# A stream's cached values move next to the following unit's stream scores

## The chip, the cores and the metric

One NeuronCore of one Trainium2 chip runs the kernel. The metric is the device time of one execution in microseconds (us); less is better. The engines are TensorE (PE, its weight loads PEld), VectorE (DVE), ScalarE (ACT), GpSimd (POOL) and SyncE (SP), which issues the DMAs. Products read SBUF and write PSUM.

## The reference, cut to what matters

One step of a hybrid encoder layer. A prompt of 1024 tokens and eight running streams of 16 new tokens each (128 stream tokens in all) are projected, attend in eight head groups ("units"), are gated, projected out and normalised. The streams attend to cached keys and values as well as to their own new ones:

```python
def band_attention_sample(q, k_new, v_new, k_cache, v_cache, rel_bias):   # units A0, A1
    k = jnp.concatenate([k_cache, k_new], axis=1)      # 128 cached rows, then 16 new ones
    v = jnp.concatenate([v_cache, v_new], axis=1)
    s = jnp.einsum('bqhd,bkhd->bhqk', q, k) * (q.shape[-1] ** -0.5) + rel_position_bias(...)
    p = jax.nn.softmax(s, axis=-1)
    return jnp.einsum('bhqk,bkhd->bqhd', p, v)

def diff_core(q, k, v, lam, mask):                     # units B0 to B3, the streams without a mask
    s = jnp.einsum('bqhmd,bkhmd->bhmqk', q, k) * (q.shape[-1] ** -0.5)
    p = jax.nn.softmax(s, axis=-1)
    w = p[:, :, 0] - lam * p[:, :, 1]
    return jnp.einsum('bhqk,bkhe->bqhe', w, v)         # diff_post scales it by its root mean square
```

Units M0 and M1 attend to 256 memory rows only. Everything is float32.

## The kernel before, in words

The eight units run in the order M0, B0, B1, B2, B3, A0, A1, M1. For each one the loop near the end of the kernel emits: the K block (`k_block`, three column chunks, 24 steps of three products, `step`, lines 155 to 157), then the V block, a gate block and the next unit's Q block as `fill`, merged with the unit's prompt attention (`attention_b`, `attention_a`, `attention_m`). V blocks transpose their chunks (`flip` in `v_block`, line 427), and gate blocks copy theirs out at line 449 into the `t1` buffers (three), the same ones that the V chunks hold until they are transposed.

The streams' attention of a unit is a list of stages from `sample` (lines 786 to 921). For a B or A unit these are: `load_k` (512 KB into the one buffer `kc`), `score(0)`, `flip`, `product(0)`, `back`, and for B also `stat` and a DMA that brings the mean squares back. `score` spreads the queries (`qz`, on POOL), multiplies the cached keys in products of 32 weight columns, one for each quarter of the array (line 806, 8 products in the source, 16 in the trace, since a float32 product runs as two), multiplies the own keys with all 128 columns (line 811), does the softmax (`soft`, into the one buffer `se`) and issues `load_v`, which puts the cached values into the same buffer `kc`. `flip` transposes the probabilities (line 863) into `pz`. `product` multiplies them with the cached values, again in products of 32 weight columns (line 891: 16 in the trace for a B unit, 32 of half the width for an A unit), then with the own values (also line 891, 128 columns), and copies the sum out (line 894). `back` transposes that (line 901) and stores it. The stages of a unit are emitted among the steps of the next unit's K block, one after every fifth step (`EV`), and what is left of them right after that block; `finish` of the unit before (its scale factors, line 523) goes behind the first of them. Those of A1 go among its own fill.

The order on each engine is the framework's: it takes whatever is ready, by the order of emission (`high_priority` moves the streams' products 100 instructions ahead). A `manual_schedule` region fixes only the order of the PE instructions inside it; others can come in between. So in a row of 32-column products there can be others, of the prompt's attention above all (lines 476, 506, 639, 678). Buffers of one tag are given out in the order in which the tiles are made: `pt` in PSUM (two buffers; all transposes, and the sum of `product`), `ps` in PSUM (three; all scores), `p` in SBUF (six; the prompt's probabilities), `t1`.

Of the kernel before, what the change touches and what calls it, by code (L numbers as in the profile page):

```python
# [15 lines left out]
P = 128  # L16
KT = 8
NTOK = 1152
NPR = 1024
# [56 lines left out]
def hybrid_step(tc, d, o):  # L76
# [331 lines left out]
    def v_block(u, blk, out, skip):  # L408

        vts = {}  # L410
        u.vdone = 0

        def evac(c, ps):
            vt = tmp.tile([P, CH], F32, tag="t1", bufs=3)
            vts[c] = vt
            nc.scalar.copy(vt, ps)
            c0 = max(skip, c * CH)
            if c0 < (c + 1) * CH:
                nc.sync.dma_start(out[:, c0 - skip : (c + 1) * CH - skip], vt[:, c0 - c * CH :])

        def flip(c):
            if c == 0:
                u.va = op_.tile([P, KT, 2, P], F32R, tag="va")
            m = npr(c) // P
            pt = ps_t.tile([P, 3, P], F32, tag="pt")
            for t in range(3):
                nc.tensor.transpose(pt[:, t], vts[c][:, t * P : (t + 1) * P], ident)  # L427
            dst = u.va[:, 3 * c : 3 * c + m]
            if u.kind == "B":
                hi, lo, src = dst[:, :, 0], dst[:, :, 1], pt[:, 0:m]  # L430
            else:
                hi, lo, src = dst[:, :, :, 0:64], dst[:, :, :, 64:128], pt[:, 0:m].rearrange("p t (h e) -> p t h e", h=2)
            nc.scalar.copy(hi, src)
            nc.vector.tensor_tensor(out=lo, in0=src, in1=f(hi), op=ALU.subtract)
            if c == 2:
                u.sv = sp.tile([P, P], F32, tag="sv")
                nc.scalar.copy(u.sv, pt[:, 2])
            u.vdone += 1

        cs = project(blk, evac)  # L440
        items = cs[0] + cs[1][:4] + [(0.35, lambda: flip(0))] + cs[1][4:]
        return items + cs[2][:4] + [(0.35, lambda: flip(1))] + cs[2][4:], [(0.35, lambda: flip(2))]
# [44 lines left out]

    def post_b(u, po, c0, n):

        od = tmp.tile([P, n], F32, tag=f"od{n}", bufs=n // P)  # L490
        nc.scalar.copy(od, po)
        hi = tmp.tile([P, 256], F32R, tag="sqh", bufs=1)
        lo = tmp.tile([P, 256], F32R, tag="sql", bufs=1)
# [292 lines left out]
    def sample(u, kc_src, vc_src, nmask):  # L786
# [3 lines left out]
        nh = 1 if kind == "B" else 2  # L790
        st = {}

        def score(t):
            if t == 0:
                for m in range(2):
                    for par in range(2):
                        src = u.sqz[m][64 * m : 64 * m + 64].rearrange("p (a b t) -> p a b t", b=2, t=16)[:, :, par]
                        nc.gpsimd.tensor_copy(qz[m][64 * par : 64 * par + 64, :, par], src)
                st["ps"] = ps_s.tile([P, 2, 256], F32, tag="ps")
            ps = st["ps"]  # L800
            kc = st["kc"]
            with tc.high_priority(offset=SP_), tc.manual_schedule(engines={PE}):

                for m in range(2):
                    for a in range(4):
                        nc.tensor.matmul(  # L806
                            ps[32 * a : 32 * a + 32, m, P * t : P * t + P], lhsT=qz[m][:, a], rhs=kc[:, m, a],
                            start=True, stop=True)
                if kind != "M":
                    for m in range(2):  # L810
                        nc.tensor.matmul(ps[:, m, 128:256], lhsT=u.sqz[m], rhs=u.sk, start=True, stop=True)
            if t == nk - 1:
                soft()
                load_v(0)
            else:
                load_k(t + 1)

        def last(tag, shape):

# [51 lines left out]

        ew = P // nh

        def product(t):
            if t == 0:
                st["po"] = ps_t.tile([P, P], F32, tag="pt")
            po, e, vc = st["po"], st["e"], st["vc"]
# [7 lines left out]
            if kind != "M":  # L885
                for h in range(nh):
                    c = slice(h * ew, (h + 1) * ew)
                    mm.append((po[:, c], e[:, h, 0:P], u.sv[:, c], False))
            with tc.high_priority(offset=SP_), tc.manual_schedule(engines={PE}):
                for x, (out, a, b, first) in enumerate(mm):  # L890
                    nc.tensor.matmul(out, lhsT=a, rhs=b, start=first, stop=(t == nk - 1 and x >= len(mm) - (4 if kind == "M" else 1)))  # L891
            if t == nk - 1:
                st["ot"] = e[:, 1, P:256]
                nc.scalar.copy(st["ot"], po)
            else:
                load_v(t + 1)

        def back():

# [2 lines left out]
            if kind == "B":  # L902
                st["sq"] = post_b(u, pt, NPR, P)
            else:
                od = u.out[:, NPR:NTOK] if u.slot == 7 else tmp.tile([P, P], F32, tag="od128", bufs=1)
# [5 lines left out]
            ms = ps_t.tile([1, P], F32, tag="pt")  # L911
            mean_square(u, st["sq"], ms, NPR, P)

        stages = [(0.0, lambda: load_k(0))] + [(0.7, lambda t=t: score(t)) for t in range(nk)] + [(0.4, flip)]
        stages += [(1.0, lambda t=t: product(t)) for t in range(nk)] + [(0.2, back)]
# [59 lines left out]
    def q_of(u):  # L975
        return q_block(u, base[u.kind][0] + u.idx, -0.125 if u.kind == "A" else 0.125)
# [176 lines left out]

    stages = []
    late = []
    first = [q_of(units[0])] + [gate_block(next(gates)) for _ in range(NG[0])]
    for row in zip(*first):
        for part in row:
            emit(part)
    for i, u in enumerate(units):  # L1160
# [149 lines left out]
```

## Time and profile before

| what | us |
|---|---|
| median of three runs | 676.22 (675.5 to 677.12) |
| the profiled execution: its time | 675.73 |
| its span, from the first to the last instruction | 673.9 |
| PE busy | 660.9 (98%) |
| mean granted TensorE clock, share of full speed | 0.996 |
| DVE, ACT, POOL busy | 473.7, 356.3, 235.1 |

The span is 1.8 us shorter than the time of the same execution. A PE row's first two figures are its start and its duration; products overlap in the array, so what one costs is the distance to the start of the next, not its duration. A row of the timeline that ends in xN stands for N like instructions in a row.

### The profile page before, as it was taken

The numbers are of one execution on the slowest core, as the hardware profiler recorded it, in microseconds if no ns is written. First come the engines' busy times: TensorE is split into PE (matmuls) and PEld (weight loads), VectorE is DVE, ScalarE is ACT, GpSimd is POOL, SyncE is SP. The second block draws the span as 40 slices with busy tenths as digits, with TensorE's granted clock in tenths as the row PEclk, the third lists the DMA queues.
The fourth block names the chain that finished last, engine by engine and source line by source line (L and its number), as shares of the span: only waits on it lengthen the run. The fifth ranks groups of instructions, "written<-read, shape, count | busy, mean of one in ns | idle before, by whom it ended". The sixth has DMA issues, their size and how long they took to land.

```text
span 673.9 us, 12216 instructions
## 1 busy us (share of the span) xinstructions
PE 660.9 (98%) x4306; PEld 614.8 (91%) x4306; DVE 473.7 (70%) x1169; ACT 356.3 (53%) x922; POOL 235.1 (35%) x282
## 2 busy tenths in 40 slices
PE   9899999999999999999999999999999999999995
PEld 8899999999999999999999999999999998887884
DVE  4869966796569856898466516675376689897854
ACT  6748855566455655566465635666466577211000
POOL 8654212541344333541234234313324124153101
PEclk9999999999999999999999999999999999999998
DMA  8771442022312222023322122031322657974411
GB/s 279 236 226 52 143 140 72 33 80 75 96 58 83 75 100 75 25 97 127 94 68 71 52 95 75 25 118 62 127 87 95 211 173 243 318 268 148 157 62 63
DMA packets 55693, 78.91 MB, mean 117 GB/s; under 512 B 9368, under 2 KB 33232, under 8 KB 55632
## 3 DMA queue, kind: packets, MB, share of 16 engines
q1 hardware_dynamic: 55632, 78.13, 35.4%
q8 instruction: 34, 0.56, 0.3%
q14 instruction: 27, 0.22, 0.1%
HBM read 57.69 MB, written 20.42 MB: 116 GB/s over the span
## 4 chain that ended last, share of the span: by engine, by line
PE 85%; DVE 7%; DMA 4%; issue 1%; ACT 1%; SPq 1%; POOL 0%; POOLq 0%; DVEq 0%; ACTq 0%
PE pp L155 16%; PE pp L156 16%; PE pp L157 16%; PE pp L1049 8%; PE ps L1049 6%; PE pt L476 4%; PE po L639 4%; PE ps L463 4%; PE ps L464 4%; PE po L678 3%; PE pt L891 1%; PE ps L806 1%; DVE xl L219 1%; DVE p L545 1%; PE pt L427 1%
## 5 line engine op out<-in xcount | busy, mean ns | idle before, releaser
L155 PE MATMUL pp<-xh,whi 128*128 128x384 f32 x616 | 211.5, 343 | 0.2 <-DVE qa L172 0.2
L156 PE MATMUL pp<-xl,whi 128*128 128x384 f32 x616 | 209.8, 341 | 1.8 <-DVE xl L219 1.8
L157 PE MATMUL pp<-xh,wlo 128*128 128x384 f32 x616 | 209.8, 341 | 0.0
L156 PEld LDWEIGHTS pp<-xl,whi 128*128 128x128 f32 x616 | 115.9, 188 | 4.6 <-DVE xl L219 2.4
L155 PEld LDWEIGHTS pp<-xh,whi 128*128 128x128 f32 x616 | 115.9, 188 | 3.2 <-issue 0.7
L157 PEld LDWEIGHTS pp<-xh,wlo 128*128 128x128 f32 x616 | 115.9, 188 | 1.6 <-issue 0.2
L140 POOL TENSOR_TENSOR wlo<-wraw,whi 128x512 fp32r<-128x512 f32 x54 | 72.4, 1362 | 65.6 <-ACT whi L139 50.4
L605 ACT ACTIVATE p<-ps,nm 128x512 f32<-128x512 f32 (+3 forms) x96 | 55.2, 580 | 47.8 <-DVE nm L602 36.2
L463 PE MATMUL ps<-ka,qa 128*128 128x512 f32 (+4 forms) x176 | 58.7, 339 | 0.5 <-DVE nm L712 0.5
L464 PE MATMUL ps<-kl,qa 128*128 128x512 f32 (+4 forms) x176 | 57.5, 328 | 0.0
L476 PE MATMUL pt<-ident,p 128*128 128x128 f32 x332 | 54.9, 274 | 0.6 <-DVE p L545 0.5
L600 DVE TENSOR_REDUCE nm<-ps 128x1 f32<-128x512 f32 (+3 forms) x96 | 51.0, 549 | 1.6
L480 DVE TENSOR_TENSOR ptl<-pt,pth 128x512 fp32r<-128x512 f32 x56 | 38.3, 684 | 10.3 <-ACT pth L479 9.7
L479 ACT CAST pth<-pt 128x512 fp32r<-128x512 f32 x56 | 32.6, 587 | 23.1 <-PE pt L476 19.9
L720 POOL TENSOR_SCALAR p<-p,rs 128x640 f32<-128x640 f32 (+4 forms) x32 | 21.5, 676 | 64.3 <-DVE rs L719 58.7
L476 PEld LDWEIGHTS pt<-ident,p 128*128 128x128 f32 x332 | 39.7, 141 | 3.9 <-DVE p L545 0.8
L1049 PE MATMUL pp<-xh,whi 128*128 128x512 f32 (+1 forms) x96 | 36.5, 381 | 0.0
L1049 PE MATMUL pp<-xl,whi 128*128 128x512 f32 (+1 forms) x96 | 36.2, 377 | 0.0
L1049 PE MATMUL pp<-xh,wlo 128*128 128x512 f32 (+1 forms) x96 | 35.9, 378 | 0.0
L639 PE MATMUL po<-pth,va 128*128 128x256 f32 (+1 forms) x160 | 35.4, 285 | 0.0
L463 PEld LDWEIGHTS ps<-ka,qa 128*128 128x128 f32 x176 | 33.2, 189 | 2.0 <-DVE nm L712 0.7
L484 DVE TENSOR_TENSOR ptl<-pt,pth 128x256 fp32r<-128x256 f32 (+1 forms) x72 | 25.1, 352 | 13.6 <-ACT pth L483 13.0
(240 smaller groups left out, 1425.0 us busy)
## 6 DMA issues: line engine op xcount, KB each, us to landing
wraw<-in_win SPq DMA_DIRECT2D x54, 256.0 KB, 3.2
xr<-in_xT SPq DMA_DIRECT2D x12, 384.0 KB, 4.6
gates<-t SPq DMA_DIRECT2D x24, 192.0 KB, 2.1
qa<-in_xn SPq DMA_DIRECT2D x9, 512.0 KB
out_y<-qa SPq DMA_DIRECT2D x16, 256.0 KB, 2.3
mixed<-od SPq DMA_DIRECT2D x28, 128.0 KB, 1.8
p<-gates SPq DMA_DIRECT2D x7, 512.0 KB
p<-mixed SPq DMA_DIRECT2D x7, 448.0 KB
```

Source lines behind the costliest of these rows:

```text
L140: eng.tensor_tensor(out=lo[:, h], in0=raw, in1=f(hi[:, h]), op=ALU.subtract)
L155: nc.tensor.matmul(ps, lhsT=w[0][:, k], rhs=xh_[:, k], start=(k == 0), stop=False)
L156: nc.tensor.matmul(ps, lhsT=w[0][:, k], rhs=xl_[:, k], start=False, stop=False)
L157: nc.tensor.matmul(ps, lhsT=w[1][:, k], rhs=xh_[:, k], start=False, stop=(k == KT - 1))
L463: nc.tensor.matmul(ps, lhsT=u.qa[h][:, qs], rhs=u.ka[h][:, k0 : k0 + n], start=True, stop=False)
L464: nc.tensor.matmul(ps, lhsT=u.qa[h][:, qs], rhs=kl[h][:, k0 : k0 + n], start=False, stop=True)
L476: nc.tensor.transpose(pt[:, t, q * P : (q + 1) * P], p[q][:, cols[t][q] : cols[t][q] + P], ident)
L480: nc.vector.tensor_tensor(out=lo, in0=pt, in1=f(hi), op=ALU.subtract)
L600: nc.vector.tensor_reduce(out=nm[:, m, c : c + 1], in_=ps[c][:, : b - a], axis=AX.X, op=ALU.max, negate=True)
L605: nc.scalar.activation(e[:, a:b], ps[c][:, : b - a], AF.Exp, bias=nm[:, m, 0:1], accum_out=rs[:, m, c : c + 1])
L639: nc.tensor.matmul(out, lhsT=a, rhs=b, start=(g == 0 and x == 0), stop=(g == j and x == len(mm) - 1))
L1049: nc.tensor.matmul(y, lhsT=a[:, k], rhs=b[k][:, s], start=(k == 0 and x == 0), stop=(k == KT - 1 and x == 2))
```

## The change

For the B and A units the second half of the stages (cached values, own values, `back`, the B units' `stat` and DMA) no longer follows the unit's own scores. It is kept in `values` and done with the next unit's stages: `load` issues the K load and the earlier unit's V load; `both` puts the earlier unit's 32-column value products, the unit's 32-column score products, its own scores and the earlier unit's own values into one region, in this order, and copies the earlier unit's sum out; `after` does the earlier unit's `back` and then the unit's softmax; `flip` and the earlier unit's `stat` and DMA follow. B0's scores have nothing ahead of them, and A1 ends with a stage for its own values. The V load goes to a `p` buffer, no longer to `kc`. `sv` gets two buffers, `ms` and `r0` three, and the small `od` tiles join the two `od256` buffers. `finish` of a B unit comes one unit later. The M units' stages stay as they were.

```diff
-                u.sv = sp.tile([P, P], F32, tag="sv")
+                u.sv = sp.tile([P, P], F32, tag="sv", bufs=2)
...
-        od = tmp.tile([P, n], F32, tag=f"od{n}", bufs=n // P)
+        od = tmp.tile([P, 256], F32, tag="od256")[:, :n]
...
-        row = tmp.tile([9, P], F32, tag="od128", bufs=1)
+        row = tmp.tile([9, P], F32, tag="od256")
...
-        u.ms = small.tile([P, 9], F32, tag="ms", bufs=2)
-        u.r0 = small.tile([P, 9], F32, tag="r0", bufs=2)
+        u.ms = small.tile([P, 9], F32, tag="ms", bufs=3)
+        u.r0 = small.tile([P, 9], F32, tag="r0", bufs=3)
...
         def load_v(t):
-            st["vc"] = vc = last("kc", [P, 8, P])
+            st["vc"] = vc = last("kc", [P, 8, P]) if kind == "M" else pp.tile([P, 8, P], F32, tag="p")
...
+        v = Unit()
+        v.load, v.cols, v.own, v.close, v.back = lambda: load_v(0), lambda: product_cols(0), product_own, close, back
+        v.rest = []
         if kind == "B":
-            stages.append((0.0, stat))
-            stages.append((0.0, lambda: nc.sync.dma_start(u.ms, mscr[u.idx].rearrange("t c -> c t"))))
-            late.append((0.1, lambda: finish(u)))
-            return stages
+            v.rest = [(0.0, stat), (0.0, lambda: nc.sync.dma_start(u.ms, mscr[u.idx].rearrange("t c -> c t")))]
+            v.finish = [(0.1, lambda: finish(u))]
+        else:
+            v.finish = []
+        prev = values[:]
+        values[:] = [v]
+
+        def load():
+            load_k(0)
+            for w in prev:
+                w.load()
+
+        def both():
+            spread()
+            tensor(
+                *[w.cols for w in prev], lambda: score_cols(0), score_own, *[w.own for w in prev])
+            for w in prev:
+                w.close()
+
+        def after():
+            for w in prev:
+                w.back()
+            soft()
+
+        stages = [(0.0, load), (1.2, both), (0.2, after), (0.4, flip)]
+        for w in prev:
+            stages += w.rest
+            late.extend(w.finish)
+        if u.slot == 1:
+            stages += [(0.0, v.load), (1.0, lambda: (tensor(v.cols, v.own), v.close())), (0.2, v.back)]
         return stages
...
             if i == 6:
+                ended = late[:]
+                late.clear()
                 stages = sample_of(u)
+                stages = stages[:LW] + ended + stages[LW:]
                 fill = fill[:ES] + with_stages(fill[ES:], EV)
```

`spread`, `score_cols`, `score_own`, `product_cols`, `product_own` and `close` are the parts of the old `score` and `product`, with the same instructions; `tensor` is the old region with `high_priority` around them.

## Rows read from the trace of the kernel before

**Rows 1.** The page, part 1: busy time, share of the span, instructions.
```profile
PE 660.9 (98%) x4306; PEld 614.8 (91%) x4306; DVE 473.7 (70%) x1169; ACT 356.3 (53%) x922; POOL 235.1 (35%) x282
```
**Rows 2.** PE's waits: engine, line, releaser; us in total, times, longest.
```profile
PE po L678 <- DVE tab L663: 0.6, 1, 0.6
```
**Rows 3.** Tile kc, PE alone: duration ns min/median/max, first and last start us, forms.
```profile
L891 PE MATMUL pt<-kc,pz x192: 219/219/297, 88.0 to 515.5; 128*32 128x64 f32 x128, 128*32 128x128 f32 x64
L806 PE MATMUL ps<-kc,qz x128: 272/273/298, 67.9 to 489.9; 128*32 128x128 f32 x128
```
**Rows 4.** Timeline, PE, B0's values: start us, us, operation, count.
```profile
168.45 0.34 PE L155 MATMUL pp<-xh,whi 128*128 128x384 f32 x1
168.63 0.34 PE L156 MATMUL pp<-xl,whi 128*128 128x384 f32 x1
168.90 0.64 PE L891 MATMUL pt<-kc,pz 128*32 128x128 f32 x16
169.47 0.27 PE L506 MATMUL po<-sqh,mean 128*1 128x256 f32 x1
169.58 0.38 PE L891 MATMUL pt<-sv,se 128*128 128x128 f32 x2
```
**Rows 5.** Timeline, PE, M1's scores.
```profile
584.48 1.08 PE L806 MATMUL ps<-p,qz 128*32 128x128 f32 x32
585.50 0.50 PE L1049 MATMUL ps<-xl,whi 128*128 128x512 f32 x1
```
**Rows 6.** Timeline, PE, B1's scores.
```profile
214.94 0.64 PE L806 MATMUL ps<-kc,qz 128*32 128x128 f32 x16
215.51 0.71 PE L811 MATMUL ps<-sk,sqz 128*128 128x128 f32 x4
```
**Rows 7.** Timeline, PE, B1's values.
```profile
243.22 0.34 PE L157 MATMUL pp<-xh,wlo 128*128 128x384 f32 x1
243.49 0.62 PE L891 MATMUL pt<-kc,pz 128*32 128x128 f32 x10
244.05 0.28 PE L506 MATMUL po<-sqh,mean 128*1 128x256 f32 x1
244.25 0.42 PE L891 MATMUL pt<-kc,pz 128*32 128x128 f32 x6
244.60 0.28 PE L506 MATMUL po<-sql,mean 128*1 128x256 f32 x1
244.72 0.39 PE L891 MATMUL pt<-sv,se 128*128 128x128 f32 x2
```
**Rows 8.** Timeline, PE, A0's scores, their first and last piece.
```profile
440.57 0.41 PE L806 MATMUL ps<-kc,qz 128*32 128x128 f32 x4
...
443.24 0.41 PE L806 MATMUL ps<-kc,qz 128*32 128x128 f32 x2
```
**Rows 9.** Timeline, PE: B2's first prompt scores, B1's flip and back, B2's V flip.
```profile
228.28 0.22 PE L463 MATMUL ps<-ka,qa 128*128 128x128 f32 x1
...
239.22 0.38 PE L863 MATMUL pt<-ident,se 128*128 128x128 f32 x2
...
249.13 0.27 PE L901 MATMUL pt<-ident,se 128*128 128x128 f32 x1
...
253.99 0.38 PE L427 MATMUL pt<-ident,t 128*128 128x128 f32 x2
```
**Rows 10.** Timeline, ACT, the same stretch.
```profile
230.33 0.30 ACT L404 COPY sk<-t 128x128 f32<-128x128 f32 x1
...
254.59 0.49 ACT L449 ACTIVATE t<-pp 128x384 f32<-128x384 f32 x1 [1.61 <-PE pt L427]
```
**Rows 11.** Timeline, DVE, the same stretch.
```profile
223.36 0.96 DVE L534 SCALAR_TENSOR_TENSOR se<-se,ri 128x256 f32<-128x256 f32 x1
...
235.68 0.66 DVE L480 TENSOR_TENSOR ptl<-pt,pth 128x512 fp32r<-128x512 f32 x1
```
**Rows 12.** Line 828, the V loads of all units.
```profile
DMA to landing us min/median/max: 3.8/4.3/4.8
```

More of the change, by code (lines that the diff above doesn't have):

```diff
@@ L791, in sample, with spread, score_cols, score_own @@
         st = {}
[L793 to L816, printed above, removed]
+        def spread():
+            for m in range(2):
+                for par in range(2):
+                    src = u.sqz[m][64 * m : 64 * m + 64].rearrange("p (a b t) -> p a b t", b=2, t=16)[:, :, par]
+                    nc.gpsimd.tensor_copy(qz[m][64 * par : 64 * par + 64, :, par], src)
+            st["ps"] = ps_s.tile([P, 2, 256], F32, tag="ps")
+        def score_cols(t):
+            for m in range(2):
+                for a in range(4):
+                    nc.tensor.matmul(
+                        st["ps"][32 * a : 32 * a + 32, m, P * t : P * t + P], lhsT=qz[m][:, a], rhs=st["kc"][:, m, a],
+                        start=True, stop=True)
+        def score_own():
+            for m in range(2):
+                nc.tensor.matmul(st["ps"][:, m, 128:256], lhsT=u.sqz[m], rhs=u.sk, start=True, stop=True)
         def last(tag, shape):
@@ L872, in sample, with product_cols @@
         ew = P // nh
-        def product(t):
+        def product_cols(t):
             if t == 0:
                 st["po"] = ps_t.tile([P, P], F32, tag="pt")
-            po, e, vc = st["po"], st["e"], st["vc"]
+            po, vc = st["po"], st["vc"]
             mm = []
@@ L884, in product, with product_own, close @@
                         mm.append((po[32 * a : 32 * a + 32, c], w, vc[:, 2 * a + par, c], t == h == par == 0))
[L885 to L896, printed above, removed]
+            for x, (out, a, b, first) in enumerate(mm):
+                nc.tensor.matmul(
+                    out, lhsT=a, rhs=b, start=first, stop=(kind == "M" and t == nk - 1 and x >= len(mm) - 4))
+        def product_own():
+            for h in range(nh):
+                c = slice(h * ew, (h + 1) * ew)
+                nc.tensor.matmul(
+                    st["po"][:, c], lhsT=st["e"][:, h, 0:P], rhs=u.sv[:, c], start=False, stop=(h == nh - 1))
+        def close():
+            st["ot"] = st["e"][:, 1, P:256]
+            nc.scalar.copy(st["ot"], st["po"])
         def back():
@@ L904, in back @@
             else:
-                od = u.out[:, NPR:NTOK] if u.slot == 7 else tmp.tile([P, P], F32, tag="od128", bufs=1)
+                od = u.out[:, NPR:NTOK] if u.slot == 7 else tmp.tile([P, P], F32, tag="od256")
                 nc.vector.tensor_copy(od, pt)
@@ L912, in stat, with tensor @@
             mean_square(u, st["sq"], ms, NPR, P)
-        stages = [(0.0, lambda: load_k(0))] + [(0.7, lambda t=t: score(t)) for t in range(nk)] + [(0.4, flip)]
-        stages += [(1.0, lambda t=t: product(t)) for t in range(nk)] + [(0.2, back)]
-        if kind == "B":
-            stages.append((0.0, stat))
-            stages.append((0.0, lambda: nc.sync.dma_start(u.ms, mscr[u.idx].rearrange("t c -> c t"))))
-            late.append((0.1, lambda: finish(u)))
-            return stages
+        def tensor(*fns):
+            with tc.high_priority(offset=SP_), tc.manual_schedule(engines={PE}):
+                for fn in fns:
+                    fn()
@@ new lines, in sample, with score, product @@
+        if kind == "M":
+            def score(t):
+                if t == 0:
+                    spread()
+                tensor(lambda: score_cols(t))
+                if t == nk - 1:
+                    soft()
+                    load_v(0)
+                else:
+                    load_k(t + 1)
+            def product(t):
+                tensor(lambda: product_cols(t))
+                if t == nk - 1:
+                    close()
+                else:
+                    load_v(t + 1)
+            stages = [(0.0, lambda: load_k(0))] + [(0.7, lambda t=t: score(t)) for t in range(nk)] + [(0.4, flip)]
+            return stages + [(1.0, lambda t=t: product(t)) for t in range(nk)] + [(0.2, back)]
@@ new lines, in sample @@
+        v = Unit()
+        v.load, v.cols, v.own, v.close, v.back = lambda: load_v(0), lambda: product_cols(0), product_own, close, back
+        v.rest = []
+        if kind == "B":
+            v.rest = [(0.0, stat), (0.0, lambda: nc.sync.dma_start(u.ms, mscr[u.idx].rearrange("t c -> c t")))]
+            v.finish = [(0.1, lambda: finish(u))]
+        else:
+            v.finish = []
[5 more added lines that the diff above has]
+                w.load()
@@ new lines, in both @@
+        def both():
+            spread()
+            tensor(
[5 more added lines that the diff above has]
+                w.back()
+            soft()
+        stages = [(0.0, load), (1.2, both), (0.2, after), (0.4, flip)]
[4 more added lines that the diff above has]
+            stages += [(0.0, v.load), (1.0, lambda: (tensor(v.cols, v.own), v.close())), (0.2, v.back)]
@@ L1155, in hybrid_step @@
     late = []
+    values = []
     first = [q_of(units[0])] + [gate_block(next(gates)) for _ in range(NG[0])]
```

## The prediction

> **What bounds the kernel now.** I read the page's busy times first: PE is busy for 98% of the span [rows 1]. In PE's list of waits the longest wait past the opening is 0.6 us [rows 2], so PE is not waiting for anybody: time leaves only if PE's own instructions take less, and it comes back if PE runs dry. A busy PE is not PE at its peak, so the third view is the order of starts around the stream products, 192 value and 128 score products of 32 columns for the B and A units together with M0 [rows 3]. Twelve stretches of them belong to the B and A units (six of scores, six of values).
>
> A clean stretch costs more than its products. B0's values: from the start of the product ahead to the start of the second one behind is 0.95 us [rows 4]. Of that 0.18 is the product ahead at its usual distance, 0.11 is the one behind at its own distance. What the 16 products cost by themselves comes from a stretch of double length: 32 take 1.02 us from the first start to the next product [rows 5], 16 take 0.57 [rows 4, 6], so each further 16 add 0.45. 0.95 - 0.18 - 0.11 - 0.45 leaves 0.21 us for going in and out of 32-column products.
>
> A stretch that is broken costs more again. B1's values have one product of line 506 between the tenth and the eleventh: 1.50 us from the product ahead to the own values [rows 7], against 0.95 for the clean one with one product fewer. 1.50 - 0.95 - 0.11 = 0.44 us for one break: a second way in and out, and a cut inside the array's rounds of eight. The timeline shows eight such breaks in the twelve stretches: one each in the values of B1, B2, B3, one in the scores of B3, three in those of A0 (its four pieces lie between the two rows of [rows 8]), one in those of A1. The other six stretches are whole.
>
> **The change part by part.**
>
> Stretches: the values of B0, B1, B2, B3 and A0 go into the stretch of the next unit's scores, so twelve stretches become seven (B0's scores and A1's values stay alone). No product is added or removed. Five ways in and out go, each between 0.21 (the clean one) and 0.44 us (the break): 1.05 to 2.2 us. I take 0.25, near the clean one, since whole stretches are joined: 5 x 0.25 = 1.3 us. All of it is on the path, as PE is the bound.
>
> [...]
>
> Breaks: what can still come between the products is what is ready on PE and was emitted earlier. The joined stretch begins with the value products, whose sum needs a `pt` buffer, and these are given out in order: it can't start before the last transposes of the prompt attention have given theirs up. In B1's case that is at 235.68 + 0.66 = 236.3 us, when VectorE has read the last group [rows 11], where the scores ran at 214.94 until now [rows 6]. At that point the attention's scores are over, its last products (line 639) are ready at the same moment and go first, the mean square of its last pair (the one in [rows 7]) comes some 7 us later, and the next unit's scores and transposes stand behind the joined stretch in `ps` and `pt`. So the three values' breaks by line 506 and those by running attention should mostly go for B1 to A0; A1's stretch lies in the middle of its own attention and keeps one or two. Bounds: all eight go (3.5 us), or none goes, since a stretch of twice the length also leaves more room for one (0). I take five: 5 x 0.44 = 2.2 us.
>
> The wait that is added: B2's first prompt scores ran at 228.28 [rows 9], and now they queue for `ps` behind the joined stretch, until about 238. PE has other work there: the V chunks and the gate block. Then, in order of `pt`: the value sum is transposed (now 249.13 - 244.72 = 4.4 us after the own values [rows 7, 9]); only then may the softmax begin, since `se` is one buffer; it took from 216.2, the end of the own scores [rows 6], to 224.3 [rows 11], 8.1 us; then the flip, about 1 us; then the next unit's V transposes. The joined stretch is about 2.1 us long (1.02 for 32 products [rows 5], 0.71 for the own scores [rows 6], 0.39 for the own values [rows 7]), and starts at 236.3: 236.3 + 2.1 + 4.4 + 8.1 + 1 = 251.9, where the V transposes come at 253.99 now [rows 9]. The gate block's chunks wait for just these: the copy at 254.59 was released by them [rows 10]. So the new chain is no longer than the old one (which ran flip, values, `back`, mean square). Cost between -0.5 and several us; zero for units B1 to A0, as the chain ends 2.1 us earlier than now. For A1, where the stages sit in the middle of its own attention and there are three more of them, I allow the longest idle that the trace has in the attentions, 0.6 us [rows 2].
>
> The V loads: six, as before, each 3.8 to 4.8 us to landing [rows 12]. They leave `kc` for a `p` buffer, so they are issued when the attention's last probability tiles have been given out (about 219 us in B1's case, an estimate from the last softmax after the scores at 214.94) and land about 223, 13 us before they are needed: nothing. Without that cover a joined stretch would wait up to 4.8 us, and the scores and transposes behind it too; on SP's queue the weight loads stand behind the V load for as long as it waits for a buffer. The K loads get earlier, since `kc` is free after the scores. The `p` buffer is held until the joined stretch is done; in that time the next unit's scores have not begun, so the prompt's five others are enough, except in A1, whose attention runs on five (in the allowance above).
>
> The small edits: the copy of the own keys into the single `sk` (230.33 now [rows 10]) must wait for the own scores at about 238, and holds a `t1` buffer on ACT's side for that long; the third V chunk needs that buffer only after its 24 products, past 240. `od256` is shared by three users in place of two tags: a wait of one store at most, on ACT, which is busy for 53% [rows 1]. More buffers for `sv`, `ms`, `r0`, and the later `finish`, whose result is read only in the output stage: nothing.
>
> Sum: 675.73 (the profiled execution; 0.5 under the median) - 1.3 - 2.2 + 0.6 = 672.8 us.
>
> **The rivals.**
>
> PE runs dry behind the joined stretch (slower). The order of `pt`, `ps` and the single `se` make one chain of joined stretch, `back`, softmax, flip, V transposes. If the joined stretch starts only after the attention's last products and `finish` (239.2, where the flip stands now [rows 9]) and the softmax, now in the queue of a busier VectorE, takes 2 us longer, the V transposes come at 251.9 + 2.9 + 2 = 256.8. The gate's first copy was released at 254.5 [rows 10]; by then PE has finished both chunks that fit in PSUM. Each us past about 255 is then idle PE: 1.8 us for each of four units, 7.2 us: 675.73 - 3.5 + 7.2 = 679.4. It decides at a V transpose later than 255 on the time scale of before. For it: PE has no slack at 254 now, and the next scores start 10 us later. Against: 251.9 by the rows as they are, and one projection chunk more can be done meanwhile, because the scores that left are no longer in the way.
>
> Only the joins count (a little faster or the same): the breaks move to other places, as the scheduler slips in other ready products and a longer stretch stands open longer. 675.73 - 1.3 = 674.4, or 675.0 with the 0.6.
>
> The switch is cheap: only the way in costs anything, 168.90 - 168.63 - 0.18 = 0.09 us [rows 4], and what I read as the way out is the pipeline's end, hidden otherwise. Ten of them, 0.9 us: 675.73 - 0.9 + 0.6 = 675.4, the same. The break of 0.44 [rows 7] speaks against it. [...]
>
> It doesn't do what it says: the region fixes only an order, and if the value and the score products become ready apart, other products stand between them and twelve stretches remain: 675.7, the same. Against: both loads land long before, so both are ready together.
>
> **How the numbers follow.** Forecast 55%: 670.4 (all eight breaks gone, 0.25 a join, no allowance: 675.73 - 1.3 - 3.5 = 670.9, and joins at 0.35) to 674.2. Only the joins: 22%, half of it faster. PE runs dry: 17%, 676.5 to 687. Cheap switch and no effect: 6%, the same. A measurement of this kernel can tell 0.2%, 1.35 us, from no change. Faster: 0.55 less a little, plus 0.11: 0.64. Same: 0.11 + 0.06 + a little: 0.19. Slower: 0.17. The range of 8 in 10 runs from 670.4 to 678.0; it leaves out most of the dry PE and the end of the forecast where more is gained than the breaks hold.
>
> **What would show it.** In the timeline of the changed kernel, PE rows of 32-column value products followed at once by 32-column score products, seven stretches for the B and A units, and at most about three breaks in them. The joined stretch of B1's scores near 236 instead of 215, the V transposes no later than 255. PE's list of waits no longer than now. The prediction is wrong if PE waits for line 427 or for copies out of PSUM, if the breaks are as many as now, or if the joined stretches are no shorter than their two halves less 0.2 us each.

## The result, and the profile after

Slower by 1.5%. In the runs made side by side the kernel after takes 687.59 us (median of six, 682.89 to 689.28), the kernel before 676.89 (six, 675.50 to 677.62): a ratio of 1.015, 95% interval 1.0115 to 1.0185. The forecast was 672.8 with a range of 670.4 to 678.0. The profiled execution after took 688.81 us, its span is 687.0, against 675.73 and 673.9 before.

The page of the profile, part 1, after; it answers to [rows 1]:

```profile
PE 664.1 (97%) x4306; PEld 616.7 (90%) x4306; DVE 467.1 (68%) x1169; ACT 354.5 (52%) x922; POOL 230.8 (34%) x282
```

The span grew by 13.1 us. PE's busy time grew by 3.2 of them (the same 4306 instructions), the time in which PE has nothing to do by 9.9. Where that time lies, the windows show (busy time of each engine in each stretch, granted clock, DMA share). First before, then after; the third row of each is a part of the second:

```profile
60.00:530.00 470.00, 469.41 (x3203) 447.65 (x3202) 322.70 (x883) 276.00 (x746) 157.32 (x212) 1.00 0.26 84
530.00:600.00 70.00, 69.38 (x414) 60.60 (x413) 60.65 (x131) 36.53 (x88) 22.13 (x14) 1.00 0.74 250
550.00:560.00 10.00, 10.00 (x58) 8.89 (x57) 9.72 (x22) 9.69 (x26) 4.78 (x3) 1.00 0.43 138
```

```profile
60.00:530.00 470.00, 466.90 (x3162) 446.62 (x3161) 311.68 (x863) 271.72 (x736) 154.49 (x213) 1.00 0.27 83
530.00:600.00 70.00, 61.91 (x398) 52.80 (x397) 53.92 (x129) 36.91 (x94) 14.93 (x10) 0.95 0.60 200
550.00:560.00 10.00, 9.07 (x65) 7.82 (x66) 8.61 (x17) 7.24 (x18) 4.29 (x3) 0.69 0.45 147
```

Up to 530 us PE is nearly full in both, and after 2.5 us more are missing than before. From 530 to 600 it is 7.5 us, and there the granted clock falls too, to 0.95. PE's waits in that last window, which answer to the single line of [rows 2]:

```profile
PE po L678 <- ACT pth L483: 2.2, 1, 2.2
PE ps L463 <- ACT p L768: 1.3, 2, 0.9
PE pt L880 <- DVE ptl L484: 1.0, 1, 1.0
PE po L678 <- DVE tab L663: 1.0, 1, 1.0
...
```

These are ordinary steps of the attentions of A1 and M1, each waiting for the one before it, with too little other work left to fill the gaps. The longest of them stands right behind the last of the products of lines 155 to 157, the input projections (timeline of after, PE):

```profile
546.89 0.34 PE L157 MATMUL pp<-xh,wlo 128*128 128x384 f32 x1
549.42 0.47 PE L678 MATMUL po<-pth,va 128*128 128x128 f32 x1 [2.20 <-ACT pth L483]
```

**The stretches** came out as forecast, and better. The joined stretch of B2's values and B3's scores (timeline of after, PE: start, us, operation, count), to be held against [rows 4 to 6]:

```profile
318.30 0.28 PE L639 MATMUL po<-ptl,va 128*128 128x256 f32 x1
318.42 0.28 PE L639 MATMUL po<-pth,va 128*128 128x256 f32 x1
318.62 0.65 PE L880 MATMUL pt<-p,pz 128*32 128x128 f32 x16
319.08 0.62 PE L804 MATMUL ps<-kc,qz 128*32 128x128 f32 x16
319.63 0.71 PE L810 MATMUL ps<-sk,sqz 128*128 128x128 f32 x4
320.18 0.39 PE L886 MATMUL pt<-sv,se 128*128 128x128 f32 x2
320.33 0.31 PE L463 MATMUL ps<-ka,qa 128*128 128x128 f32 x1
```

From the product ahead to the own scores it is 319.63 - 318.42 = 1.21 us; less 0.12 for the product ahead and 2 x 0.45 for 32 products, 0.19 is left for going in and out: what one clean stretch cost before (0.21), now paid once for two halves. Twelve stretches became seven, and one break is left of eight, in B1's (two value products at 235.75, the rest from 236.87).

**The start of the next attention** is what the last line of that fence shows. B3's first prompt scores (line 463) stand behind the joined stretch, and this behind the last products of B2's attention (line 639). Before, the two attentions overlapped. Timeline of before, PE:

```profile
303.69 0.22 PE L463 MATMUL ps<-ka,qa 128*128 128x128 f32 x1
...
314.69 0.48 PE L463 MATMUL ps<-ka,qa 128*128 128x512 f32 x1
315.00 0.28 PE L639 MATMUL po<-ptl,va 128*128 128x256 f32 x1
...
315.48 0.28 PE L639 MATMUL po<-pth,va 128*128 128x256 f32 x1
```

B3's scores began at 303.69, 11.8 us ahead of the last product of B2's attention; after they begin 1.9 us behind it. So the softmax of the next attention starts late each time. Its first exponential (ACT, line 605 for B, 718 for A units), and the last one of M1 (line 768), in us:

| first exponential of | B2 | B3 | A0 | A1 | M1, last |
|---|---|---|---|---|---|
| before | 232.5 | 309.4 | 383.2 | 461.1 | 564.2 |
| after | 239.6 | 321.7 | 397.7 | 472.2 | 576.3 |
| later by | 7.1 | 12.3 | 14.5 | 11.1 | 12.1 |

### The profile page after: what moved, and what is told of

It reads as the page before. It is cut to its first block, busy times and chain, and to the rows that moved or that the text cites. A ratio compares the mean times of both kernels' runs of the same rounds, so it can differ in the third digit from the quotient of the medians.

```text
span 687.0 us, 12226 instructions
## 1 busy us (share of the span) xinstructions
PE 664.1 (97%) x4306; PEld 616.7 (90%) x4306; DVE 467.1 (68%) x1169; ACT 354.5 (52%) x922; POOL 230.8 (34%) x282
## 4 chain that ended last, share of the span: by engine, by line
PE 79%; DVE 8%; DMA 7%; ACT 3%; issue 2%; SPq 0%; POOL 0%; POOLq 0%; DVEq 0%; ACTq 0%
PE pp L155 14%; PE pp L156 14%; PE pp L157 14%; PE pp L1098 9%; PE ps L1098 6%; PE pt L476 4%; PE po L639 4%; PE ps L463 3%; PE ps L464 3%; PE po L678 3%; PE pt L880 1%; DVE t L368 1%; DMA rs<-rstd 1%; PE ps L804 1%; DMA wraw<-in_win 1%
## 5 line engine op out<-in xcount | busy, mean ns | idle before, releaser
L140 POOL TENSOR_TENSOR wlo<-wraw,whi 128x512 fp32r<-128x512 f32 x54 | 71.0, 1334 | 89.9 <-ACT whi L139 72.4
L479 ACT CAST pth<-pt 128x512 fp32r<-128x512 f32 x56 | 32.9, 587 | 24.7 <-PE pt L476 12.1
L139 ACT CAST whi<-wraw 128x512 fp32r<-128x512 f32 x54 | 30.8, 618 | 10.9 <-PE pp L156 8.5
```

Of the source, the lines that this page charges most:

```text
L140: eng.tensor_tensor(out=lo[:, h], in0=raw, in1=f(hi[:, h]), op=ALU.subtract)
L479: nc.scalar.copy(hi, pt)
```

## The experiments

Expectations name theories by a letter; this is what each says costs the time. C: A1's joined region ties the buffers of scores and transposes together in the middle of A1's own attention. S: what came along, V in `p` and the added stages. D: the late starts at the B joins; D1: only the last of them, ahead of A1, counts; D2: each adds its share. T: a late start is given back at the next boundary. H: the tie, i.e. that stream scores now wait for a `pt` buffer. L: what moved with the values. J: a B join costs something besides the tie. A unit's `slot` is 2 to 5 for B0 to B3, 0 and 1 for A0 and A1.

### Which join costs

**A0's values apart, four joins left** (edit of after):

```diff
-        values[:] = [v]
+        values[:] = [v] if u.slot != 0 else []
...
-        if u.slot == 1:
+        if u.slot < 2:
             stages += [(0.0, v.load), ...]
```

> Four of the five joins stay (B0 to B3); A0's values are done in stages of their own behind A0's flip, so A1's stretch holds scores alone. A1's list keeps as many stages as in the changed kernel. Theory C (in A1 the joined region ties the scores' queue `ps` to the transposes' queue `pt` in the middle of A1's own attention, which costs some 17 us there, while the joins elsewhere give about 4): about 673 us, 3 to 5 below the kernel before. Theory S (A1 is late because it has more stages and V tiles in `p` buffers): still about 685. Theory D (PE runs dry behind the joined stretches of the K blocks, the rival of the prediction): still about 685.

685.92 us, 1.0127 (1.0106 to 1.0147). Most of the loss, 9.0 of 10.7 us, stays without the join in A1's attention.

**Only that join** (edit of after; V loads and value stages of the others as before):

```diff
-        values[:] = [v]
+        values[:] = [v] if u.slot == 0 else []
```

> Only the values of A0 are joined, with A1's scores; the B units and M stay as in the kernel before, but for the V tiles in `p` buffers. Theory C and theory S: 688 to 693 us, the whole loss without the gain. Theory D: about 677, as the kernel before.

675.97 us, 0.9988 (0.9968 to 1.0008): no cost that can be told from none. Theory C falls. This is also the place for which the prediction set aside 0.6 us.

**A1's scores and A0's values in two regions** (edit of after):

```diff
+            if u.slot == 1:
+                tensor(lambda: score_cols(0), score_own)
+                tensor(*[w.cols for w in prev], *[w.own for w in prev])
+            else:
                 tensor(*[w.cols for w in prev], lambda: score_cols(0), score_own, ...)
```

> The changed kernel, but in A1's stage the scores are a region of their own, emitted ahead of the region with A0's values, so the scores no longer wait for a `pt` buffer; stages and buffers stay. Theory C: 672 to 676 us, most of the loss gone. Theory S: about 687. Theory D: about 687.

689.03 us, 1.0185 (1.0156 to 1.0214): the loss stays, as after the first run it had to.

**V tiles in `p`, nothing joined** (edit of before):

```diff
-            st["vc"] = vc = last("kc", [P, 8, P])
+            st["vc"] = vc = last("kc", [P, 8, P]) if kind == "M" else pp.tile([P, 8, P], F32, tag="p")
```

> The kernel before with one part of the change alone: the B and A units' V tiles go to a `p` buffer, and nothing is joined. Theory C and D: about 677 us, as before. Theory S, where the V tiles in `p` carry it: 680 to 690.

676.86 us, 1.0001 (0.9987 to 1.0014). Theory S falls for the buffer; for the added stages it falls with the kernel of A1's join alone, whose list of stages for A1 is that of the changed kernel.

**B joins in part** (edit of after; the others in stages of their own):

```diff
+        kept = u.slot in (2, 3, 4)     # then (5,), (3,), (5, 0)
-        values[:] = [v]
+        values[:] = [v] if kept else []
```

> Three joins stay: the values of B0, B1, B2 with the scores of B1, B2, B3. B3, A0 and A1 do their own values as in the kernel before. Every joined stretch holds the next unit's first prompt scores back. Theory D1 (PE covers that with projections as long as there are any, so only a late start of A1's attention, the last ones, costs): 673 to 677 us. Theory D2 (each held start costs its share of the loss): 682 to 685.

> One join stays: B3's values with A0's scores, the stretch ahead of A1's attention. Theory D1: 685 to 689 us, nearly the whole loss from this one. Theory D2: 679 to 681, a quarter of it.

> The kernel after with one join left, B1's values with B2's stream scores; all other values in their own stages, as before. It lies three attentions ahead of A1. If every late start adds its own share (theory D2), a fifth to a third of the loss stays: B3's attention starts 7 to 12 us late (316 to 321 us against 309.4), and the time is 678.5 to 681. If a delay is a debt that the next boundary without a join gives back, because its own wait has slack there (theory T), B3 starts late but A0 or A1 starts on time (A0's first exponential 383 to 386, A1's 461 to 463) and the time is 675.5 to 677.5.

> The kernel after with two joins left, those that cost nothing by themselves: B3's values with A0's scores, and A0's with A1's. From the two runs with one each (-0.9 and -0.1 us): 675.5 us, so 674.5 to 677 if they stay independent, with A1's first exponential at 460 to 463 us. If delays of neighbouring boundaries build up even here (theory D2), M1's attention starts late and it is 678 to 681.

The joins of B0, B1 and B2: 682.19 us, 1.0082 (1.0065 to 1.0099). B3's alone: 676.37, 0.9997 (0.9979 to 1.0015). B1's alone: 680.29, 1.0049 (1.0034 to 1.0065). B3's and A0's: 676.56, 0.9995 (0.9981 to 1.0008). D1 falls: the last B join costs nothing by itself, an early one costs 3.5 us. D2 has the right direction (it expected 682 to 685 for the joins of B0 to B2), but not for B3's, whose joined stretch at 451.6 us left A1's first exponential where it was (461.9 against 461.1). T falls for B1's join: B3 starts at 319.4, A0 nearly on time at 384.3, and yet A1 at 466.2 and 3.5 us are lost.

### The tie by itself

**Stream scores that take a `pt` buffer, nothing joined, nothing moved** (edit of before; the second kernel has it at B2's scores alone, `u.slot == 4`):

```diff
+            held = t == 0 and u.slot in (0, 1, 3, 4, 5)
+            if held:
+                hold = ps_t.tile([P, P], F32, tag="pt")
             with tc.high_priority(offset=SP_), tc.manual_schedule(engines={PE}):
+                if held:
+                    nc.tensor.transpose(hold, ident, ident)
                 for m in range(2):
...
+            if held:
+                nc.scalar.copy(small.tile([P, 1], F32, tag="hold", bufs=1), hold[:, 0:1])
```

> The kernel before, with one thing added: at the five places where the joined stretch stands in the kernel after (the stream scores of B1, B2, B3, A0 and A1), the region of the stream scores also takes a tile of the transposes' buffer, pt, and writes it with one 128x128 transpose ahead of the scores. No values move, no loads move, the softmax stays where it was; the output is the same. Theory H (what costs is the tie: scores that must wait for a pt buffer come after the previous attention's last transposes, and the next unit's prompt scores queue behind them in ps): the stream scores move from 215, 290, 366 and 441 us to within some 5 us of the next unit's first softmax exponential, A1's first exponential comes at 466 to 473 us against 461.1, and the time is 682 to 689 us though nothing was joined. Rival L (what costs is what moved with the values: the load into p, the close and the transpose back ahead of the softmax): A1's first exponential at 461 to 462 and 676 to 678 us, the five transposes at 0.3 us each.

> The kernel before with the tie at one place alone, the stream scores of B2, where the one join of an earlier run (680.3 us, +3.5) stood; nothing is joined or moved. Theory H: B3's first exponential at 317 to 323 us against 309.4, and the whole cost of that one join, 679 to 682 us. If the join's cost came from what it moved, 676 to 677.5.

At all five places: 695.57 us, 1.0284 (1.0252 to 1.0316). B1's scores moved from 214.94 [rows 6] to this place (timeline of the kernel with five ties, PE):

```profile
240.04 0.28 PE L639 MATMUL po<-pth,va 128*128 128x256 f32 x1
240.16 0.27 PE L523 MATMUL pt<-ident,ms 128*9 128x128 f32 x1
240.27 0.27 PE L807 MATMUL pt<-ident 128*128 128x128 f32 x1
240.47 0.65 PE L810 MATMUL ps<-kc,qz 128*32 128x128 f32 x16
241.04 0.71 PE L815 MATMUL ps<-sk,sqz 128*128 128x128 f32 x4
241.51 0.31 PE L463 MATMUL ps<-ka,qa 128*128 128x128 f32 x1
```

It is the order of the kernel after without a single joined product: last products of the attention, the transpose into the added `pt` tile, the stream scores, and only then the next unit's first prompt scores. A1's first exponential comes at 479.5 us, and 18.8 us are lost. The transpose itself is 0.2 us from start to start. That is more than H expected (682 to 689 us), and more than the kernel after loses. One thing differs from it: each unit's own values still follow its held scores, and B2's V transposes (line 427) come at 256.09, where they stood at 253.99 before [rows 9] and stand at 251.04 after. So the 18.8 us show that the tie is enough to cost time, not what it costs inside the kernel after.

At B2's scores alone: 680.30 us, 1.0054 (1.0039 to 1.0068). The kernel with the join at the same place took 680.29. In both, B3's attention starts right behind the last products of B2's (line 639), and its first exponential within 2 us of the other's. First with the tie (PE, ACT), then with the join (PE, ACT):

```profile
314.86 0.28 PE L639 MATMUL po<-pth,va 128*128 128x256 f32 x1
314.98 0.27 PE L523 MATMUL pt<-ident,ms 128*9 128x128 f32 x1
315.09 0.27 PE L807 MATMUL pt<-ident 128*128 128x128 f32 x1
315.29 0.64 PE L810 MATMUL ps<-kc,qz 128*32 128x128 f32 x16
...
316.33 0.31 PE L463 MATMUL ps<-ka,qa 128*128 128x128 f32 x1
```

```profile
317.76 0.38 ACT L605 ACTIVATE p<-ps,nm 128x128 f32<-128x128 f32 x1
```

```profile
316.53 0.28 PE L639 MATMUL po<-pth,va 128*128 128x256 f32 x1
316.74 0.53 PE L880 MATMUL pt<-p,pz 128*32 128x128 f32 x11
...
318.44 0.31 PE L463 MATMUL ps<-ka,qa 128*128 128x128 f32 x1
```

```profile
319.44 0.37 ACT L605 ACTIVATE p<-ps,nm 128x128 f32<-128x128 f32 x1
```

### The join without the tie

**B1's join alone, its sum in a scores buffer** (edit of the kernel with B1's join; the output tile is taken apart from the probabilities and the softmax put ahead of the transpose back; the second kernel uses a projections' buffer, `ps_p`, tag `pp`):

```diff
-                st["po"] = ps_t.tile([P, P], F32, tag="pt")
+                st["po"] = ps_t.tile([P, P], F32, tag="pt") if u.slot != 3 else ps_s.tile([P, P], F32, tag="ps")
...
-            st["ot"] = st["e"][:, 1, P:256]
+            st["ot"] = st["e"][:, 1, P:256] if kind == "M" else tmp.tile([P, 256], F32, tag="od256")[:, :P]
...
+            soft()
             for w in prev:
                 w.back()
-            soft()
```

> The one join of B1's values with B2's scores again, with its sum in a scores buffer in place of one of the transposes, the output tile apart and the softmax ahead of the transpose back. With the sum in pt this join cost 3.5 us (680.3), and so did the tie alone at this place. Theory H (the tie is all that a B join costs): B3's first exponential at 304 to 311 us, 675.5 to 677.5. Theory J (a B join costs something besides, which hid behind the tie): on time and all the same 678.5 to 681.

> The same one join with its sum in a projections' buffer. Theory H: 675.5 to 677.5 with B3's first exponential at 304 to 311 us, if PE does not wait for the V load there; with a wait of 1.5 us as in the run of five such joins, up to 678.5. Theory J: 678.5 to 681.5. If it and the run beside it differ by over 2 us, the cost lies in the buffer that the sum takes away, not in the join.

Sum in `ps`: 677.31 us, 0.9999 (0.9979 to 1.0018). The 3.5 us are gone. Its timeline, PE and ACT:

```profile
301.96 0.64 PE L880 MATMUL ps<-p,pz 128*32 128x128 f32 x16
302.42 0.38 PE L804 MATMUL ps<-kc,qz 128*32 128x128 f32 x2
302.78 0.77 PE L476 MATMUL pt<-ident,p 128*128 128x128 f32 x5
303.48 0.64 PE L804 MATMUL ps<-kc,qz 128*32 128x128 f32 x14
304.04 0.71 PE L810 MATMUL ps<-sk,sqz 128*128 128x128 f32 x4
304.59 0.39 PE L886 MATMUL ps<-sv,se 128*128 128x128 f32 x2
304.74 0.30 PE L463 MATMUL ps<-ka,qa 128*128 128x128 f32 x1
```

```profile
307.82 0.37 ACT L605 ACTIVATE p<-ps,nm 128x128 f32<-128x128 f32 x1 [1.46 <-DVE nm L600]
```

The stretch runs 13.7 us earlier than with the sum in `pt` (there its first two products ran at 315.62), in the middle of the old attention, whose transposes (line 476) break it once; B3's first exponential comes at 307.8 against 309.4 before. So at this one place the tie is the whole price of the join: put in alone it costs 3.3 us (680.30 against 676.99), and taken out of the join it brings the ratio from 1.0049 to 0.9999. (The output tile and the order of softmax and transpose back changed along with it, and weren't tried by themselves.)

Sum in `pp`: 682.18 us, 1.0077 (1.0048 to 1.0106), more than either theory allowed. Here another cover is gone. SP's queue and PE:

```profile
295.12 0.34 SPq L401 DMA_DIRECT2D out_bkT<-t  x1
295.51 0.92 SPq L822 DMA_DIRECT2D p<-in_cbv  x2
```

```profile
291.64 0.28 PE L506 MATMUL po<-sql,mean 128*1 128x256 f32 x1
299.32 1.08 PE L880 MATMUL pp<-p,pz 128*32 128x128 f32 x16 [7.40 <-DMA p<-in_cbv]
300.15 1.11 PE L804 MATMUL ps<-kc,qz 128*32 128x128 f32 x16
```

The stretch now stands in PE's queue before its V tile is there. The V load is issued at 295.51, right behind a store (line 401) that itself went out only at 295.12, and PE waits 7.4 us for it. With the sum in `ps` the V load goes out at 295.57, no earlier, but there the stretch begins only at 301.96. The prediction named this cost for a lost cover, at up to 4.8 us, and rightly held it to be covered as long as the stretch waits for `pt`; it came out larger.

**All the B joins without the tie** (the same edit on after, for all units or for the B units; the last expectation is of a kernel in which every `both` has two regions, as A1's had above, the scores first):

> All five joins in one region as in the changed kernel, but the value sum goes to one of the projections' two PSUM buffers (`pp`) instead of `pt`, and is copied to an `od256` tile, so that the softmax is emitted ahead of `back`. The joined stretch then waits for no transposes. Theories D1 and D2: 671 to 675 us, the gain of the joins without the held scores. If a taken `pp` buffer stalls the projections, or the loss lies elsewhere: 680 and more.

> The five joins of the kernel after in one stretch each, but the sum of the values in a buffer of the scores (ps) in place of one of the transposes (pt), the output tile apart from the probabilities, and the softmax ahead of the transpose back. The stretch then waits for nothing of the transposes, as in the run with the sum in a projection buffer, but no projection buffer is held. Theory H (the tie to pt costs): the stretches lie at 215 to 220, 290 to 298, 366 to 374 us, A1's first exponential comes at 453 to 462 us, and, if holding the projections' buffer was what spoilt the other run, the time is 673 to 679 us. If it is 683 to 687 again with early starts, early starts are not enough, and what costs is something that both these runs have: the late landing of the V load at the stretch, or the end of the program.

> The four joins of B's values (with the scores of B1, B2, B3 and A0), with the sum in a scores buffer as in the run before, and A0's values and A1's scores each in a stage of its own, with the sum in pt. Theory H (the tie to pt behind the B joins is what costs, and what was left in the run before, 683.1 us, comes from the sum in ps in the middle of A1's attention, whose joined stretch was broken there: 48 products in 3.1 us): the next units start on time (232 to 234, 305 to 311, 377 to 385, A1 at 456 to 463 us), PE idles under 4 us after 60 us, and the time is 673 to 677.5. Theory J (the B joins cost something besides the tie, in the loads into p or in the buffers of the scores they hold): on time and all the same 679 to 683.

> All five joins, the sum of B's values in a scores buffer and A0's in a transposes' buffer as in the kernel after, where that join by itself cost nothing. Theory H: as the run beside it, less the 0.9 us at most that the A1 join gained alone: 672.5 to 677.5. Theory J: 679 to 683. If this one stays at 681 to 685 and the one beside it comes to 673 to 677.5, it is the join in A1's attention, wherever its sum lies, once the softmax stands ahead of the transpose back.

> The changed kernel with the order of stages and buffers as it is, but in every unit the scores are a region ahead of the region with the values, so scores need no `pt` buffer and stretches aren't joined. Theories D1 and D2: 676 to 680 us, the loss gone and the gain of the joins too. If the loss comes from the later values or from the softmax behind `back`: still 685 to 689.

| kernel | us | ratio (95%) | first exponential A1 | M1, last | PE idle past 60 us |
|---|---|---|---|---|---|
| before | 676.89 | | 461.1 | 564.2 | 1.2 |
| after | 687.59 | 1.0150 (1.0115 to 1.0185) | 472.2 | 576.3 | 11.2 |
| five ties alone | 695.57 | 1.0284 (1.0252 to 1.0316) | 479.5 | 579.6 | 14.3 |
| five joins, sums in `pp` | 685.02 | 1.0135 (1.0118 to 1.0152) | 453.7 | 576.3 | 11.9 |
| five joins, sums in `ps` | 683.10 | 1.0100 (1.0070 to 1.0129) | 458.7 | 568.0 | 7.3 |
| four B joins in `ps`, A0's apart | 681.27 | 1.0063 (1.0043 to 1.0084) | 460.1 | 567.6 | 7.1 |
| the same, A0's joined in `pt` | 689.89 | 1.0193 (1.0163 to 1.0224) | 460.2 | 577.0 | 12.9 |
| scores first, values in a region behind | 701.01 | 1.0367 (1.0347 to 1.0388) | 469.7 | 587.3 | 17.1 |

Each of these kernels was run beside kernels before of its own (medians 676.48 to 676.99), to which the ratios refer. The starts are on time with the sums in `ps` or `pp`, as H says, and 4.3 to 12.9 us stay lost all the same: against H's expectation, and for J as far as several joins go. The four B joins lost 9.0 us with the tie (685.92, A0's values apart) and lose 4.3 without it (681.27): there the tie is about half of the loss. With `pp`, 3.2 us of PE's wait are for the V loads of two stretches. With `ps`, a stretch holds two of the three scores buffers at each of four boundaries, and the waits of the kernel with four B joins are of another kind (PE on the copies out of PSUM, line 450: 2.7 us). That these buffers are the cause wasn't tried with several joins. The last kernel was slower than any theory had it. There the softmax stands behind the values, and the scores keep their `ps` buffer until then: B2's first exponential is early (225.0), its last late (306.9 against 294.5). Nor is it settled why A0's join, free by itself, costs 8.6 us beside four B joins in `ps`; no theory expected it. The traces place the loss: from A1's first exponential to its last it is 79.7 us with that join and 69.0 without, and M1's first exponential comes at 540.8 in place of 529.9. The kernel that was free had its transpose back ahead of the softmax and this one behind it.

## Why the prediction was wrong

**The bound** was read rightly: time comes back when PE runs dry, and it did, by 9.9 us of 13.1.

**Stretches and breaks**: right in number and more: all five joins were made, and seven breaks are gone where five were forecast. By the prediction's own prices that is 5 x 0.25 + 7 x 0.44 = 4.3 us, against the 3.5 of the sum; the total doesn't show it apart, and at the single place with the tie removed no gain can be told from none (0.9999, 0.9979 to 1.0018). What makes up the 0.44 us of a break, the trace of before shows: B0's 16 value products start in four groups of four, 0.11 to 0.13 us from one group to the next (a round of eight is two such groups, each product being there twice); those of B1 start in groups of four, four, one and one, and behind the product of line 506 of three and three. By estimate that is two groups more, 2 x 0.11 = 0.22 us; the rest, 0.22, is near the 0.21 of a second way in and out.

**The wait that is added** is the step that failed. Its times were right at the place for which they were worked out: B1's joined stretch began at 235.75 (forecast 236.3), B2's first prompt scores at 238.57 (forecast about 238), and the V transposes came earlier than in [rows 9]. Timeline of after, PE:

```profile
250.16 0.38 PE L857 MATMUL pt<-ident,se 128*128 128x128 f32 x2
...
251.04 0.55 PE L427 MATMUL pt<-ident,t 128*128 128x128 f32 x3
```

251.04 was forecast as 251.9. But the step put the price at zero because "PE has other work there", the V chunks and the gate block, and by the times below that work was not free: what fills PE while an attention is held is missing later, where the attention needs something beside it. The price of the held starts was not zero: with the tie alone it is 3.3 us at one place and 18.8 at five.

In the kernel after, most of the lack shows at the end. The last input projection (lines 155 to 157) starts at 546.89 instead of 552.31, while M1's last exponential moved from 564.2 to 576.3: the stretch of attention without input projections grew from 11.9 to 29.4 us. (Products of the output, line 1049 before and 1098 after, fill a part of it in both.) In the kernel with the tie at B2's scores alone that stretch is as long as before, from 556.29 to 568.4, and half of the added idle time lies some 13 to 17 us behind the held scores (timeline, PE):

```profile
325.64 0.34 PE L157 MATMUL pp<-xh,wlo 128*128 128x384 f32 x1
...
330.92 0.51 PE L427 MATMUL pt<-ident,t 128*128 128x128 f32 x3
...
333.83 0.44 PE L155 MATMUL pp<-xh,whi 128*128 128x384 f32 x1
```

No input projection starts between 325.64 and 333.83, and from 318 to 334 us PE is idle for 1.7 us; before, the projections ran on up to the V transposes at 329.99 and behind them, and PE was idle for 0.03 us in the same window. So a held start does show as idle PE near its place once the work beside it is used up; in the kernel with five ties 6.5 us of idle PE lie in 60 to 530 us and 7.8 in 530 to 600 (before 0.6 and 0.6). That the used-up work is what costs the time is read from these times; no run tried it by itself.

**The allowance** of 0.6 us for A1 stood at the wrong place: that join alone measured -1.0 us, no change that can be told (0.9968 to 1.0008).

**The V loads** were covered, as forecast: B0's is issued at 213.98 (forecast about 219) for a stretch at 235.75. The moved tile cost nothing (1.0001), and the price of lost cover appeared only where the stretch no longer waited for `pt`.

**The rivals.** "PE runs dry behind the joined stretch" had the right sign and the right engine, but its deciding point, V transposes later than 255, was not met: they came at 251. In the kernel after, the chain through `pt`, `se` and the V transposes wasn't the one that counted. What counted was the chain of prompt attentions, whose overlap (11.8 us from B2 to B3) was given up. In the kernel with one tie the rival is nearer: there PE does run short of work behind the held stretch, until the projections go on at 333.83, though the V transposes come only 0.9 us later than before (330.92 against 329.99). "It doesn't do what it says" and "only the joins" are excluded by the seven stretches, six of them whole and one broken once. Whether the switch is cheap, the totals can't say.

What stays open: how the loss is shared among several boundaries (B3's join costs nothing alone, 3.5 us belong to B1's, and five ties cost more than five times 3.3), and why four B joins without the tie still lose 4.3 us. So the tie is shown as the cause at B2's scores, and as about half of the loss at the four B joins; the rest of the 10.7 us is open.

## What to carry to other kernels

If an operation is moved behind a wait, list what queues behind it in each buffer it holds, and follow that work to the end of the program: a full engine at the place of the delay may only mean that other work was brought forward. Compare where the filling work ends with where the chain that needs it ends, at the next boundary and at the end of the program; here the chain was the later one already (552.3 and 564.2 us), so there was little filling work to lend. A region that takes two kinds of buffers starts with the later of them, and so ties together queues that were free of each other: test this with a kernel that takes the buffer and moves nothing, and check what else queues behind it there.

## What the runs showed of the hardware

In two kernels the granted clock was lower behind a long wait of PE. In the kernel after, PE waited for 2.20 us up to 549.42 and for 1.03 us up to 550.92; the granted clock was 1.00 up to 549, 0.71 in 549 to 550, 0.50 from 550 to 556, 0.88 in 556 to 557 and 1.00 again from 557 on; over 550 to 560 us it was 0.69, where it was 1.00 before. The longer of these waits began 40.9 us behind the start of the last joined stretch (506.34). PE's busy time in the whole program grew by 3.2 us with the same instructions; how much of this is the clock's wasn't separated. In the kernel of B1's join with the sum in `pp`, PE waited for 7.40 us up to 299.32; there the granted clock was 0.85 in 290 to 300 and 0.81 in 300 to 310 us, and the 32 products of its stretch took 1.86 us from the first start to the own scores in place of 1.01 (318.62 to 319.63 in the kernel after).

The joined stretch of B2's values and B3's scores shows no pause between value and score products of 32 columns: the first score product starts 0.46 us after the first of 16 value products, where a further 16 cost 0.45 in [rows 5].
